# A row softmax limited by its transfers: loads of 3 to 32 rows and stores of up to 16, in place of sixteen equal chunks of 8

## The chip, the cores and the metric

The kernel runs on one core of one Trainium2 chip. The metric is device microseconds of one execution. The kernel before takes 163.15 us (median of the first 3 runs, 162.96 to 163.39). Four engines matter here: DVE (VectorE, the maxima and the scaling), ACT (ScalarE, the exponentials), the DMA engines (16 of them, which carry the loads and the stores), and SP, which only issues the loads. The stores are issued by ACT. The TensorE is not used; the granted clock was 1.0.

The profile's span is about 1.8 us shorter than the device time (161.3 us against 163.08 us in the profiled run). Times inside the program are counted from the span's start.

## The reference

```python
def setup_inputs():
    batch, seq, dim = 16, 1024, 512
    return {"x": np.random.randn(batch, seq, dim).astype(np.float32)}

def reference(x):
    x_max = np.max(x, axis=-1, keepdims=True)
    exp_x = np.exp(x - x_max)
    return (exp_x / np.sum(exp_x, axis=-1, keepdims=True)).astype(np.float32)
```

That is a softmax over 512 numbers for 16,384 rows. A core has 128 partitions, so each partition gets 128 rows of 2 KB. In all, 33.55 MB are read and 33.55 MB written. Below, "8 rows" means 8 rows in each of the 128 partitions: 2 MB in all, 16 KB per partition.

## The kernel before

```python
CHUNKS = [8] * 16
SLOTS = {8: 12}
...
    def load(k):                       # SP issues; 16 KB per partition
        tiles[k] = data.tile([P, R, d], F32, ..., bufs=SLOTS[R])
        nc.sync.dma_start(out=tiles[k], in_=src[k])

    def rowmax(k):                     # DVE: one instruction for 8 rows
        nc.vector.reduce_max(out=shift[k], in_=tiles[k], axis=AX, negate=True)

    def exps(k):                       # ACT: one instruction per row, with its sum
        for r in range(R):
            nc.scalar.activation(out=tiles[k][:, r, :], in_=tiles[k][:, r, :], func=EXP,
                bias=shift[k][:, r : r + 1], accum_out=sums[k][:, r : r + 1], ...)

    def scale(k):                      # DVE: reciprocal, then one product per row
        ...
    def store(k):                      # ACT issues
        nc.scalar.dma_start(out=dst[k], in_=tiles[k])

    with tc.manual_schedule():
        for k in range(K):
            load(k); rowmax(k); exps(k)
            if k >= 1:
                scale(k - 1); store(k - 1)
        scale(K - 1); store(K - 1)
```

Twelve chunks of 16 KB per partition, 192 KB, are held at a time.

Of the kernel before, what the change touches and what calls it, by code (L numbers as in the profile page):

```python
# [1 line left out]

# [4 lines left out]

F32 = mybir.dt.float32
EXP = mybir.ActivationFunctionType.Exp
AX = mybir.AxisListType.X  # L10


CHUNKS = [8] * 16

SLOTS = {8: 12}


@with_exitstack
def kernel(
    ctx: ExitStack,  # L20
    tc: tile.TileContext,
    x: bass.AP,
    out: bass.AP,
):
    nc = tc.nc
    P = nc.NUM_PARTITIONS

    x_flat = x.flatten_outer_dims()
    out_flat = out.flatten_outer_dims()
    n, d = x_flat.shape  # L30
    assert n == P * sum(CHUNKS)


    src, dst, at = [], [], 0
    for R in CHUNKS:
        for flat, views in ((x_flat, src), (out_flat, dst)):
            part = flat[at : at + P * R, :]
            views.append(part.rearrange("(p r) d -> p r d", r=R))
        at += P * R

    data = ctx.enter_context(tc.tile_pool(name="data", bufs=1))
    stats = ctx.enter_context(tc.tile_pool(name="stats", bufs=4))

    K = len(CHUNKS)
    tiles = [None] * K
    shift = [None] * K
    sums = [None] * K

    def load(k):
        R = CHUNKS[k]  # L50
        tiles[k] = data.tile([P, R, d], F32, name=f"x{R}", tag=f"x{R}", bufs=SLOTS[R])
        nc.sync.dma_start(out=tiles[k], in_=src[k])  # L52

    def rowmax(k):
        R = CHUNKS[k]
        shift[k] = stats.tile([P, R], F32, name=f"shift{R}", tag=f"shift{R}")
        nc.vector.reduce_max(out=shift[k], in_=tiles[k], axis=AX, negate=True)  # L57

    def exps(k):
        R = CHUNKS[k]  # L60
        sums[k] = stats.tile([P, R], F32, name=f"sums{R}", tag=f"sums{R}")
        for r in range(R):
            nc.scalar.activation(  # L63
                out=tiles[k][:, r, :],
                in_=tiles[k][:, r, :],
                func=EXP,
                bias=shift[k][:, r : r + 1],
                scale=1.0,
                accum_out=sums[k][:, r : r + 1],
            )  # L70

    def scale(k):
        R = CHUNKS[k]
        recip = stats.tile([P, R], F32, name=f"recip{R}", tag=f"recip{R}")
        nc.vector.reciprocal(out=recip, in_=sums[k])  # L75
        for r in range(R):
            nc.vector.tensor_scalar_mul(  # L77
                out=tiles[k][:, r, :],
                in0=tiles[k][:, r, :],
                scalar1=recip[:, r : r + 1],  # L80
            )

    def store(k):
        nc.scalar.dma_start(out=dst[k], in_=tiles[k])  # L84

    with tc.manual_schedule():
        for k in range(K):
            load(k)
            rowmax(k)
            exps(k)  # L90
            if k >= 1:
                scale(k - 1)
                store(k - 1)
        scale(K - 1)
        store(K - 1)


# [1 line left out]
_INS = ['x']  # L99
_OUTS = [((16, 1024, 512), 'float32')]  # L100


# [23 lines left out]
```

## Time and profile before

| | value | where it is read |
|---|---|---|
| span | 161.3 us | page |
| DMA busy | nine tenths or more in 38 of 40 slices | page, DMA row |
| DVE, ACT busy | 77%, 58% | page |
| bytes moved | 67.1 MB, about 431 GB/s in a full slice | page |
| 16 KB piece on one DMA engine | 611 ns; the next begins 607 ns after it began | the trace's DMA packets |
| last store issued | 149.49 us | timeline |

These are lines of the profile page of the kernel before: the span, two engines' busy time, the busy tenths of the DMA engines and the GB/s in 40 equal slices of 4.03 us, and the packets, MB and share of each queue (q1 the loads, q10 the stores).

```profile
span 161.3 us, 527 instructions
...
DVE 123.8 (77%) x160; ACT 93.2 (58%) x257; POOL 0.2 (0%) x4
...
DMA  6999999999999999999999999999999999999993
GB/s 163 431 427 427 431 435 378 418 445 431 423 439 431 421 435 431 431 439 418 439 435 427 431 427 435 435 425 435 431 427 439 431 427 427 431 435 431 431 435 171
...
q1 hardware_dynamic: 2304, 33.56, 49.5%
q10 hardware_dynamic: 2304, 33.56, 48.6%
```

The reader should see that the DMA engines are never without work between the first and the last slice, and that the rate is the same with loads alone (slices 2 to 6), with both, and with stores alone (the last seven). The small dip to 378 GB/s in slice 7 is where the first store joins.

The next line is the page's chain of work that ended last, by engine, as shares of the span.

```profile
DMA 52%; DVE 31%; ACT 6%; SPq 2%; issue 1%; ACTq 1%; DVEq 0%
```

The chain goes back from the last instruction, and the time that a store spends in its queue after it was issued is not one of its steps. The timeline of the kernel before shows that time; its columns are start, duration, engine, source line, operation, tiles.

```profile
22.40 0.37 ACTq L84 DMA_DIRECT2D out_dram<-x  x1
...
146.19 3.26 DVE L77 TENSOR_SCALAR x<-x,recip 128x512 f32<-128x512 f32 x8
...
149.49 0.34 ACTq L84 DMA_DIRECT2D out_dram<-x  x1
```

The last store is issued at 149.49 us and moves 2 MB, which takes 4.9 us at 431 GB/s. It does not start until about 154 us, because earlier stores are still in the queue. DVE could have ended some 3 us later without loss (an estimate: these 4.5 us, less the 1.0 us from the first load's issue to its first piece). So DVE is not the limit; the DMA engines are.

### A budget of one DMA engine

For a kernel of this kind I need a finer account than the page. The trace has one record for each piece that a DMA engine moves: start, duration, size and queue (the recorded texts below call a piece a packet). One partition's contiguous run is one piece, so a chunk of 8 rows makes 128 pieces of 16 KB, 8 on each engine. The engine's number is not recorded; I joined pieces to 16 engines by the end of one and the start of the next. A few pieces are joined wrongly (the bytes of an engine come out up to a few per cent off 4.19 MB), so the means over the 16 engines are good and a single engine's figure is approximate.

The budget has these terms, in us per engine, as means over 16, and together with the 1.74 us before the first piece they make the mean end: the usual time of all its pieces (each size's usual duration, less the 4 ns by which pieces overlap); "slow", by how much pieces took longer than is usual for their size; idle gaps; and "spread", by how much the last engine ends after the mean.

```
kernel          pieces  usual   slow   gaps   mean end  spread  last engine's end   span
before            256   155.39  1.58   0.47    159.19    0.98        160.17        161.3
```

Of the 1.58 us of slow pieces, 0.92 lie in the first 4 us and 0.53 where the first store joins at 24.6 to 28 us.

### The profile page before, as it was taken

What the parts mean: (1) busy time and instruction counts of PE and PEld (TensorE: products, weight loads), DVE (VectorE), ACT (ScalarE), POOL (GpSimd) and SP (SyncE); (2) the same over time, 40 slices, a digit from 0 to 9 for tenths busy, and PEclk for the clock granted to TensorE, in tenths of its full rate; (3) what the DMA queues carried; (4) which work ended last, traced back from release to release, by engine and by line L of the source; (5) the groups of instructions that cost most, each with busy time, mean ns of one, the idle gap of its engine ahead of it and who ended that gap; (6) DMA issues with size and microseconds to landing.
All of it is one profiled execution on the core that took longest, in us unless ns stands there. A gap on an engine that the chain in (4) does not pass through costs nothing.

```text
span 161.3 us, 527 instructions
## 1 busy us (share of the span) xinstructions
DVE 123.8 (77%) x160; ACT 93.2 (58%) x257; POOL 0.2 (0%) x4
## 2 busy tenths in 40 slices
DVE  0088799999999999985970079999999999957000
ACT  0037994959596867067002996859595959591000
POOL 0000000000000000000000000000000000000000
DMA  6999999999999999999999999999999999999993
GB/s 163 431 427 427 431 435 378 418 445 431 423 439 431 421 435 431 431 439 418 439 435 427 431 427 435 435 425 435 431 427 439 431 427 427 431 435 431 431 435 171
DMA packets 4612, 67.14 MB, mean 416 GB/s; under 512 B 513, under 2 KB 513, under 8 KB 513
## 3 DMA queue, kind: packets, MB, share of 16 engines
q1 hardware_dynamic: 2304, 33.56, 49.5%
q10 hardware_dynamic: 2304, 33.56, 48.6%
q14 instruction: 4, 0.02, 0.0%
HBM read 33.55 MB, written 33.55 MB: 416 GB/s over the span
## 4 chain that ended last, share of the span: by engine, by line
DMA 52%; DVE 31%; ACT 6%; SPq 2%; issue 1%; ACTq 1%; DVEq 0%
DMA x<-in_x_dram 52%; DVE shift L57 16%; DVE x L77 14%; ACT x L63 6%; SPq L52 2%; DVE recip L75 1%; ACTq L84 0%; DVEq L121 0%; ACTq L63 0%
## 5 line engine op out<-in xcount | busy, mean ns | idle before, releaser
L63 ACT ACTIVATE x<-x,shift 128x512 f32<-128x512 f32 x128 | 90.5, 709 | 44.1 <-DVE shift L57 21.4
L57 DVE TENSOR_REDUCE shift<-x 128x8 f32<-128x4096 f32 x16 | 70.6, 4415 | 9.7 <-DMA x<-in_x_dram 9.7
L77 DVE TENSOR_SCALAR x<-x,recip 128x512 f32<-128x512 f32 x128 | 52.1, 482 | 0.6
L63 ACT ACTIVATION_READ_ACCUMULATOR x<-x,shift 128x1 f32 x128 | 24.0, 187 | 0.0
L75 DVE RECIPROCAL recip<-sums 128x8 f32<-128x8 f32 x16 | 3.1, 196 | 15.3 <-ACT x L63 15.3
L63 ACT ACT_TABLE_LOAD x1 | 1.3, 1283 | 8.7 <-DMA x<-in_x_dram 8.7
L110 POOL MEMSET const-bfloat16-1.0<- 128x1 bf16 x1 | 0.1, 102 | 0.0
L110 POOL MEMSET const-uint8-127<- 128x1 uint8 x1 | 0.1, 102 | 0.0
L110 POOL MEMSET const-float32-0.0<- 128x1 f32 x1 | 0.1, 99 | 0.2 <-issue 0.2
L110 POOL MEMSET const-float32-1.0<- 128x1 f32 x1 | 0.1, 99 | 0.0
## 6 DMA issues: line engine op xcount, KB each, us to landing
x<-in_x_dram SPq DMA_DIRECT2D x16, 2048.0 KB, 42.6
out_dram<-x ACTq DMA_DIRECT2D x16, 2048.0 KB, 18.0
```

The costliest lines, as they stand in the source:

```text
L52: nc.sync.dma_start(out=tiles[k], in_=src[k])
L57: nc.vector.reduce_max(out=shift[k], in_=tiles[k], axis=AX, negate=True)
L63: nc.scalar.activation(out=tiles[k][:, r, :], in_=tiles[k][:, r, :], func=EXP, bias=shift[k][:, r : r + 1], scale=1.0, accum_out=sums[k][: ...
L75: nc.vector.reciprocal(out=recip, in_=sums[k])
L77: nc.vector.tensor_scalar_mul(out=tiles[k][:, r, :], in0=tiles[k][:, r, :], scalar1=recip[:, r : r + 1],)
L110: nc = _bacc.Bacc("TRN2", target_bir_lowering=False, num_devices=1)
```

## The change

The intent is to start computing and storing earlier (a first load of 3 rows), to move the bulk in fewer, larger transfers, and to hold everything in one array of 192 KB per partition, whose first 32 rows are reused by the last two chunks.

```diff
-CHUNKS = [8] * 16
-SLOTS = {8: 12}
+CHUNKS = [   # rows, place in the array
+    (3, 0), (5, 3), (8, 8), (16, 16), (32, 32), (32, 64), (16, 0), (16, 16),
+]
+SBUF_ROWS = 96
+EARLY = 6                             # loads issued at the start
+AFTER_STORE = {2: [6], 3: [7]}        # load 6 after the store of chunk 2, 7 after 3
+GROUP = 8                             # rows computed at a time
+FINISH_BEFORE = (1, 2, 3)             # chunks 0 to 2 are finished before the next begins
+STORE_ROWS = {4: 16, 5: 16}           # the 32-row chunks are stored by 16
 ...
+    held = data.tile([P, SBUF_ROWS, d], F32, name="held")
+    place = [held[:, s : s + R, :] for R, s in CHUNKS]
 ...
     def load(k):
-        tiles[k] = data.tile([P, R, d], F32, ..., bufs=SLOTS[R])
-        nc.sync.dma_start(out=tiles[k], in_=src[k])
+        nc.sync.dma_start(out=place[k], in_=src[k])
 ...        # rowmax, exps and scale now work on a group g of 8 rows (or 3, or 5)
+        if since is not None:         # end of the group: rows since..b are stored
+            nc.scalar.dma_start(out=dst[k][:, since:b, :], in_=place[k][:, since:b, :])
+        if b == CHUNKS[k][0]:
+            for later in AFTER_STORE.get(k, ()):
+                load(later)
 ...
+        for k in range(EARLY):
+            load(k)
+        waiting = None
+        for g, (k, a, _, _) in enumerate(groups):
+            if waiting is not None and a == 0 and k in FINISH_BEFORE:
+                scale(waiting)
+                waiting = None
+            rowmax(g)
+            exps(g)
+            if waiting is not None:
+                scale(waiting)
+            waiting = g
+        scale(waiting)
```

The compute is the same but for one more maximum and one more reciprocal. Comments in this diff are mine.

## The prediction

> **What bounds the kernel now.** The DMA engines, end to end. In the page's 40 slices the DMA row reads 9 in all but the first and last, at about 431 GB/s, whether loads, stores or both are moving. It moves 67.1 MB: 155.5 of 161.3 us. DVE is busy 77%, ACT 58%. A 16 KB packet begins 607 ns after the one before on its engine; 256 per engine make 155.4 us. The rest: first packet at 1.74 us, about 0.9 us of slow first packets, 0.5 us of slow packets where the first store joins (25 to 26.5 us), 1.3 us to the last landing, 0.8 us to the end. Loads end at 132 us; then a backlog of stores drains: the last (2 MB) is issued at 149.5 us (timeline) and starts near 154 us.
>
> The long waits (ACT 12.1 us for a load, whose semaphore a store reuses) cost nothing: the DMA was never without work.
>
> **What the change does.** Same bytes, same 192 KB, nearly the same DVE and ACT work. It removes packets: loads of up to 64 KB and stores of up to 32 KB per partition, 144 instead of 256 per engine. It moves the first store from 22.4 us to about 11.3 us (3 rows land near 5.6, maximum 1.75, exps 2.1, scale 1.4); that fills no hole, as loads fill the engines then. It adds: chunks 0 to 3 run one by one, so 16 rows are done at about 34 us (before: some 20); loads 6 and 7 wait for stores; the last store is 4 MB, 9.7 us instead of 4.9.
>
> The Trainium skill ("DMA: Bandwidth & Descriptors", section "Where 436 GB/s comes from") gives a ceiling of 435 GB/s; the trace shows 431 to 432. 16 KB at the ceiling is 602 ns, so a packet's own cost is an estimated 5 ns: 112 fewer save an estimated 0.55 us, all critical.
>
> **Is DVE still in time?** An estimate from its durations: 7.735 us for 8 rows (timeline, 97 to 140 us), 16 rows at 34 us, so last maximum ends near 137.3 us (before 140.1), last store issued near 146.8 us. By then the DMA, if never idle, nears row 224 of 256 (loads plus stores), which ends near 148.5 us; a first packet comes 1.0 us or more after issue. The last store arrives just in time, margin about 1 us. The first 32-row load must also beat the small stores: the same page ("Queues, rings and completion order") says engines alternate between queues per packet, and the trace shows load, store, load, store. With 64 KB load packets against 6 to 10 KB stores it lands near 46 us, needed at 47.8. If split into 32 KB, near 50, and DVE ends 2 us later.
>
> **Prediction.** 162.5 us, range 161.3 to 164.6: a gain of about 0.6 us, the risk lying above. Faster by over 2% 0.05, within 2% 0.89, slower 0.06.
>
> **Right or wrong, in the profile.** DMA row 9 throughout, 431 to 435 GB/s; first store issued at 11 to 12 us; DVE ends at 146 to 149 us; no dip before the last store.
>
> **What would make it wrong.** A rate that depends on packet size (64 KB strides in HBM); a dip between 65 and 90 us where loads 6 and 7 wait; the one-by-one start; the last store late by several us.

## The result, and the profile after

The changed kernel takes 164.49 us (median of 4 runs, 164.45 to 164.67) against 163.17 us (4 runs). The ratio is 1.0083, with a 95% interval of 1.0065 to 1.0100. A ratio in this document is worked out from the fast runs of both kernels in the same rounds, so it is not quite the ratio of the medians. The change is thus 0.8% slower: within 2%, but of the opposite sign to the forecast.

The same lines of the page after (the slices are 4.07 us here), with the chain's shares in the last line:

```profile
span 162.7 us, 510 instructions
...
DVE 124.0 (76%) x162; ACT 93.3 (57%) x257; POOL 0.2 (0%) x4
...
DMA  5999997979889799899999999999999999999991
GB/s 203 433 475 387 402 559 311 561 333 543 335 356 540 330 403 542 346 387 467 403 403 379 395 475 419 397 483 411 427 451 411 459 435 395 475 427 395 475 419 56
...
q1 hardware_dynamic: 1152, 33.55, 49.3%
q10 hardware_dynamic: 1440, 33.56, 48.0%
...
DVE 55%; DMA 28%; ACT 3%; issue 3%; SPq 1%; DVEq 0%; ACTq 0%
```

Two readings are traps. First, the chain of waits went from DMA 52% to DVE 55%, as if DVE had become the limit. It had not: DVE's busy time is the same (124.0 against 123.8 us), and the last store is issued earlier than before. Second, the GB/s row jumps between 311 and 561. A 64 KB piece takes 2.4 us on one engine and is counted whole in one slice, so this row cannot be read for such pieces. If each piece's bytes are spread over its own duration, the rate between 24 and 36 us is 429 to 433 GB/s.

Here is the timeline after: the first store, the only longer wait of DVE for a load once it is under way, and the end.

```profile
10.74 0.37 ACTq L103 DMA_DIRECT2D out_dram<-held  x1
...
48.72 4.42 DVE L75 TENSOR_REDUCE shift<-held 128x8 f32<-128x4096 f32 x1 [2.01 <-DMA held<-in_x_dram]
...
144.27 3.26 DVE L97 TENSOR_SCALAR held<-held,recip 128x512 f32<-128x512 f32 x8
...
147.56 0.34 ACTq L103 DMA_DIRECT2D out_dram<-held  x1
```

The first store comes 11.7 us earlier than before, and the last one 1.9 us earlier. The engines are not idle before it: its first pieces start at 149.5 us, right behind the store ahead of it. Compute is not what got slower.

The budget shows where the time went:

```
kernel          pieces  usual   slow   gaps   mean end  spread  last engine's end   span
before            256   155.39  1.58   0.47    159.19    0.98        160.17        161.3
after             144   154.83  2.77   0.46    159.80    1.65        161.45        162.7
difference       -112   -0.56  +1.19  -0.01     +0.61   +0.67         +1.28         +1.4
```

The saving that the change is made for, fewer pieces, is there: 0.56 us. It is more than eaten by slow pieces (+1.19 us per engine) and by the spread of the engines' ends (+0.67 us). The slow time, by period: 0.42 us in the first 8 us (before: 0.92 in the first 4), 0.34 at 12 to 24 us, 0.16 at 32 to 40, 0.44 at 40 to 48, 0.21 at 56 to 64, 0.41 at 76 to 84 and 0.66 at 84 to 88 us. It lies on load pieces almost alone (2.51 of 2.77 us), and nearly all of it comes before 88 us, while the loads go on to 117 us.

This listing, made from the trace's DMA packets, shows three of the engines at 82 to 89 us. L is a piece of a load and S one of a store, with its size in KB and its start; the bracket is by how many ns it was slow; a point is the small write that reports a transfer done.

```
L32@81.2 S32@82.4 L32@83.6 . L32@84.9(+631) S32@86.7 L32@87.9 S32@89.1
S32@82.0 L32@83.2 S32@84.4 L32@85.6(+802) S32@87.6 L32@88.8
S32@82.1 L32@83.3 S32@84.5 L32@85.7(+1318) . L32@88.3 S32@89.5
```

All the engines stall over the same two or three microseconds, but not by the same amount. Since each engine has its own fixed 4.19 MB to move, an engine that stalls more stays behind to the end. When the records are joined so that each piece is followed by the one that starts nearest to 4 ns before its end, 12 of the 16 engines come out at exactly 144 pieces. In this joining the two engines that end near 161.4 us have 3.6 and 3.8 us of slow pieces, and the eleven that end before 159.7 us have 2.2 to 2.6 us. So in the changed kernel the spread is not a second cause: it is the same slow time, unevenly shared.

What makes pieces slow? Three theories went into the experiments. A: the large load pieces. B: the order of work (small chunks first, one by one; late loads 6 and 7). C: the late 4 MB last store. Theory A was sharpened on the way; the letters D to G stand for theories that the recorded expectations below name.

### The profile page after: what moved, and what is told of

It is laid out like the page before. It is cut to its first block, busy times and chain, and to the rows that moved or that the text cites. A ratio compares the mean times of both kernels' runs of the same rounds, so it can differ in the third digit from the quotient of the medians.

```text
span 162.7 us, 510 instructions
## 1 busy us (share of the span) xinstructions
DVE 124.0 (76%) x162; ACT 93.3 (57%) x257; POOL 0.2 (0%) x4
## 4 chain that ended last, share of the span: by engine, by line
DVE 55%; DMA 28%; ACT 3%; issue 3%; SPq 1%; DVEq 0%; ACTq 0%
DVE shift L75 30%; DMA held<-in_x_dram 28%; DVE held L97 24%; ACT held L83 3%; SPq L70 1%; DVE recip L95 1%; DVEq L149 0%; ACTq L83 0%
## 5 line engine op out<-in xcount | busy, mean ns | idle before, releaser
L83 ACT ACTIVATE held<-held,shift 128x512 f32<-128x512 f32 x128 | 90.5, 708 | 45.5 <-DVE shift L75 39.6
L75 DVE TENSOR_REDUCE shift<-held 128x8 f32<-128x4096 f32 (+2 forms) x17 | 70.6, 4159 | 7.2 <-DMA held<-in_x_dram 7.2
L97 DVE TENSOR_SCALAR held<-held,recip 128x512 f32<-128x512 f32 x128 | 52.2, 480 | 0.6
L83 ACT ACTIVATION_READ_ACCUMULATOR held<-held,shift 128x1 f32 x128 | 23.9, 187 | 0.0
L95 DVE RECIPROCAL recip<-sums 128x8 f32<-128x8 f32 (+2 forms) x17 | 3.3, 192 | 15.8 <-ACT held L83 15.8
```

The costliest lines, as they stand in the source:

```text
L75: nc.vector.reduce_max(out=shift[g], in_=place[k][:, a:b, :], axis=AX, negate=True)
L83: nc.scalar.activation(out=place[k][:, r, :], in_=place[k][:, r, :], func=EXP, bias=shift[g][:, r - a : r - a + 1], scale=1.0, accum_out=s ...
L95: nc.vector.reciprocal(out=recip, in_=sums[g])
L97: nc.vector.tensor_scalar_mul(out=place[k][:, r, :], in0=place[k][:, r, :], scalar1=recip[:, r - a : r - a + 1],)
```

## The experiments

All runs below gave correct results. "Slow" and "spread" are the terms of the budget in the run that was profiled.

```
kernel      median us  ratio to before    pieces  slow   gaps   spread  last engine
before       163.15                         256   1.58   0.47    0.98     160.17
after        164.49   1.0083                144   2.77   0.46    1.65     161.45
l8           171.84   1.0533                216   2.62   8.82    0.10     168.44
s8           166.39   1.0201                200   2.60   0.57    3.85     163.87
ls8          163.08   0.9997                272   1.52   0.58    0.73     159.99
b35          163.21   1.0004                272   1.62   0.52    0.90     160.22
l16          162.69   0.9979                160   1.18   0.60    0.97     159.42
start8       164.83   1.0105                128   2.82   0.45    2.12     161.89
nodry        165.31   1.0135                160   2.62   0.59    2.46     162.32
bsplit       163.52   1.0024                264   1.90   0.57    1.07     160.71
cut5         164.49   1.0084                152   2.13   0.54    1.92     161.18
cut4         163.29   1.0017                152   1.58   1.00    0.89     160.06
l16dry       162.60   0.9973                160   1.33   0.49    1.00     159.43
l16start8    162.56   0.9967                144   1.49   0.79    0.69     159.53
first64      164.56   (one look)            104   1.77   3.17    0.10     161.42
best8        162.64   0.9967                152   1.50   0.45    0.98     159.53
best35       162.95   0.9980                168   1.45   0.46    1.25     159.83
best64       162.38   0.9959                112   1.64   0.45    0.83     159.33
best64b      162.89   0.9985                128   2.29   0.36    0.92     160.06
small64      163.96   1.0052                128   3.03   0.38    2.41     162.33
```

Some cautions. The ratios' intervals are about 0.0013 wide to each side. Only l8 is slower by a clear 2%; s8 lies at that limit, and all the other differences are smaller. The runs were made on four chips, each beside the kernel before, whose medians there lay between 163.06 and 163.13 us. And the profiled run of small64 was the slowest of its six (165.25 us against a median of 163.96), so its slow and spread terms together are about 1.3 us too large for a typical run. l16start8 and best8 each had one execution near 167 us, which the ratios leave out as slow.

### 1. Cut the loads, the stores, or both to 8 rows

The edits to the changed kernel: for the loads,

```diff
-        nc.sync.dma_start(out=place[k], in_=src[k])
+        for a in range(0, R, 8):
+            b = min(R, a + 8)
+            nc.sync.dma_start(out=place[k][:, a:b, :], in_=src[k][:, a:b, :])
```

and for the stores `STORE_ROWS = {3: 8, 4: 8, 5: 8, 6: 8, 7: 8}`. Run l8 has the first, s8 the second, ls8 both.

> Changed kernel, with every load cut into pieces of at most 8 rows (16 KB packets); memory layout, order, stores untouched. Budget of one DMA engine so far: packets slower than the usual time of their size cost 1.58 us in the kernel before and 2.77 us in the changed one; the last engine ends 0.98 us after the mean of the 16 before and 1.65 us after. Theory A (large load packets cause the slow packets): they fall to 1.0 to 1.6 us, packets' own cost rises 0.35 us, time about 163.5 us. Rival B (order of work, small first chunks, late loads are the cause): slow packets stay near 2.7, time 164.5 +-0.3 us.

> Changed kernel, with every store cut to at most 8 rows (16 KB packets); loads keep 32 KB and 64 KB packets. Theory A: slow packets of the loads stay (2.3 us or more per engine), the spread of the engines' ends falls from 1.65 to about 1.0 us, time about 163.9 us. Rival B: both stay, 164.5 +-0.3 us. Rival C (the 4 MB last store is issued too late): time falls as well, but then the trace should show the store queue empty before the last store.

> Changed kernel, loads and stores both cut to at most 8 rows; array, places, DRAM layout, order of compute untouched. Theory A: slow packets about 1.0 to 1.6 us and spread about 1.0 us per engine, time 162.7 to 163.2 us, that is as before or a little better. Rival B: 164.5 +-0.3 us. Rival D (64 KB stride between partitions in DRAM, not packet size, makes the loads slow): slow packets stay at 2.3 us or more, time near 164.2 us.

Measured: 171.84, 166.39 and 163.08 us. Each half of the edit does harm, and both together bring back the time of the kernel before. Theory A had forecast the time of ls8 (162.7 to 163.2 us), but no theory had forecast that each half alone does harm. B is out as the main cause, because ls8 has the small chunks, the order and the late loads of the changed kernel and is 1.4 us faster. D is out too: ls8 reads with the same 64 KB stride between partitions, and is not slow.

l8 shows what inequality can do in the extreme. The engines alternate between the two queues piece by piece (between 60 and 70 us, 93% of the joined pieces follow one of the other queue), so 16 KB loads beside 32 KB stores get about one third of the engine. Between 64 and 68 us the pieces show 135 GB/s of loads and 297 GB/s of stores (in the kernel before: 248 and 183). The loads fall behind and DVE has to wait for them, here in l8's timeline:

```profile
135.37 4.42 DVE L78 TENSOR_REDUCE shift<-held 128x8 f32<-128x4096 f32 x1 [3.87 <-DMA held<-in_x_dram]
...
143.87 4.42 DVE L78 TENSOR_REDUCE shift<-held 128x8 f32<-128x4096 f32 x1 [0.67 <-DMA held<-in_x_dram]
...
154.39 3.26 DVE L100 TENSOR_SCALAR held<-held,recip 128x512 f32<-128x512 f32 x8
```

and the stores that wait for DVE leave the DMA engines empty. The view by windows of l8 gives start and end, length, busy time of DVE, ACT and POOL with counts, the clock, the DMA's busy share and its GB/s:

```profile
128.00:136.00 8.00, 4.10 (x11) 5.75 (x16) 0.00 (x0) 1.00 0.99 428
...
140.00:144.00 4.00, 3.33 (x9) 4.00 (x11) 0.00 (x0) 1.00 0.18 78
```

That is the 8.8 us of gaps in the table, and it explains l8's time. It is not what happens in the changed kernel, which has no such gaps.

s8 is the opposite case: 64 and 32 KB loads beside 16 KB stores. Its engines always have work (gaps 0.57 us), it is slow to the same amount as the changed kernel (2.60), but its last engine ends 3.85 us after the mean. Why its spread is more than twice that of the changed kernel at about the same slow time is not shown. Theory C finds nothing there: the stores run without a break to the end.

### 2. The small start in the kernel before

Run b35 gives the kernel before the chunks 3, 5 and fifteen of 8; run bsplit cuts only its first load into 3 and 5 rows.

```diff
-CHUNKS = [8] * 16                 # b35
+CHUNKS = [3, 5] + [8] * 15
-        nc.sync.dma_start(out=tiles[k], in_=src[k])      # bsplit
+        for a, b in ((0, 3), (3, 8)) if k == 0 else ((0, R),):
+            nc.sync.dma_start(out=tiles[k][:, a:b, :], in_=src[k][:, a:b, :])
```

> Kernel before, with its first 8-row chunk cut into 3 and 5 rows, nothing else. The slow packets of the first 4 us cost 0.92 us per engine before and 0.42 us with the changed kernel's small first loads. If small first packets are the reason, this gives 162.6 to 162.8 us. If the small stores that follow disturb the stream, or the 3 and 5 row start does nothing by itself, 163.2 us or more.

> Kernel before with its first load cut into 3 and 5 rows, its chunk and its store left whole. The kernel before with 3 and 5 row chunks won 0.44 us per engine in the first 4 us and lost 0.43 us where three small first stores, not one, joined. If that is so, the win is kept here: slow packets 1.1 us per engine instead of 1.58, time 162.6 to 162.8 us, under both kernels. If not, 163.1 us.

Measured: 163.21 and 163.52 us, no gain. In b35 the slow pieces of the start fall from 0.92 to 0.48 us, but 1.01 us appear at 12 to 28 us. In bsplit the start costs 0.64 us, and the one first store, unchanged in size and moment, now costs 1.15 instead of 0.53 us. So my expectation for bsplit was wrong: what is won at the start is lost when the store queue joins. Start and first stores together cost 1.5 to 1.8 us in the kernel before and in these two. Why is not shown.

### 3. No load piece over 32 KB

Run l16 cuts the two 32-row loads of the changed kernel into pieces of 16 rows (the loop above with 16 for 8); cut5 does it for the second alone, cut4 for the first alone.

> Changed kernel with its two 32-row loads cut into pieces of 16 rows, so that no load packet is over 32 KB, as no store packet is; all else as changed. Theory A1 (it is the inequality of load and store packets: 64 KB loads beside small stores): slow packets from 36 to 62 us (0.9 us per engine with the changed kernel) go, those at 77 to 87 us (1.0 us), where both are 32 KB, stay; 163.7 to 164.2 us. Theory A2 (size of load packets as such): both shrink, 163.3 us. Rival: loads get a smaller share against the first stores, the second 16-row piece lands late, DVE waits, and time rises over 164.7 us.

> Changed kernel, only the second of its two 32-row loads cut into 16-row pieces (no cut: 164.49 us; both cut: 162.69 us). Theory A2 (each 64 KB load packet stream does its own harm): about half of the gain, 163.3 to 163.9 us, with the slow packets of 43 to 47 us (0.44 us per engine) kept and those of 58 to 62 us gone. Rival E (what matters is only that loads 6 and 7 are issued before the load queue runs empty): time follows the moment of load 6's issue; if the queue still runs empty, 164.2 us or more.

> Changed kernel, only the first of its two 32-row loads cut into 16-row pieces. Theory A2: 163.3 to 163.9 us, slow packets of 43 to 47 us gone or halved. Rival E: as for the other half; the first store lands earlier than in the changed kernel, so load 6 is issued earlier, and if the load queue then does not run empty the time is near 162.7 us although one 64 KB load is left.

Measured: l16 takes 162.69 us, 1.8 us less than the changed kernel and faster than the kernel before (0.9979, interval 0.9965 to 0.9992). Slow pieces fall from 2.77 to 1.18 us and the spread to 0.97 us. Even those at 77 to 87 us are gone, where both the changed kernel and l16 move 32 KB loads beside 32 KB stores. I had expected them to stay, so they look like an after-effect of the 64 KB pieces before them; no run shows that by itself.

Cutting the second of the two 64 KB loads alone changes nothing (cut5, 164.49 us, with 0.43 us at 43 to 47 us kept), so one load of 64 KB pieces beside a small store is enough for the whole loss. By the times of the pieces, that first 32-row load (23.8 to 48 us) runs beside the store of 5 rows (28.6 to 49 us, pieces of 10 KB); the store of 3 rows is over at 24.9 us. Cutting the first alone gives 163.29 us. This does not show that the second load is harmless beside a small store: in cut4 it moves at 51.4 to 78.9 us, when the store of 8 rows is over at 52.6 us, and so it meets the 32 KB pieces of the next store instead.

### 4. The order: the start of 8, and a load queue that runs empty

Run start8 joins the first two chunks of the changed kernel to one of 8 rows. nodry loads chunk 6 in two halves, so that the load queue does not run empty at 72 us. l16dry is l16 with loads 6 and 7 both held back until chunk 3 is stored, which was meant to make the load queue run empty. l16start8 is l16 with the start of 8.

```diff
-    (3, 0), (5, 3), (8, 8), (16, 16), ...      # start8, l16start8
+    (8, 0), (8, 8), (16, 16), ...              # and the indices that follow from it
-    ... (32, 64), (16, 0), (16, 16),           # nodry
+    ... (32, 64), (8, 0), (8, 8), (16, 16),
-AFTER_STORE = {2: [6], 3: [7]}
+AFTER_STORE = {1: [6], 2: [7], 3: [8]}
-    ... (32, 64), (16, 0), (16, 16),           # l16dry
+    ... (32, 64), (16, 16), (16, 0),
-AFTER_STORE = {2: [6], 3: [7]}
+AFTER_STORE = {3: [6, 7]}
```

> Changed kernel with its first two chunks (3 and 5 rows) joined to one of 8. If the 6 and 10 KB stores among 64 KB loads make the slow packets of 13 to 47 us, those (about 1.1 us per engine) fall by half or more, while the slow first 4 us return (0.9 instead of 0.4 us): 164.0 us. If they don't matter, slow packets rise by 0.5 us: 164.9 us. The last store is issued about 1 us earlier or at the same time (147.5 us), which decides nothing.

> Changed kernel with the load of chunk 6 (16 rows) cut into two chunks of 8, of which the first waits for the stores of the first 8 rows alone (landed at 51.5 us), so that the queue of loads does not run empty at 72 us, as it does in the changed kernel. If a restart of an empty load queue makes the slow packets of 77 to 80 us (0.41 us per engine), they go, and perhaps those of 83 to 87 us (0.66) too: 163.5 to 164.1 us. If not, 164.5 +-0.3 us.

> The fast version (loads of at most 16 rows, 162.69 us), with the places of the last two chunks exchanged, so that load 6 waits for the store of chunk 3 (landed at 78 us) while the loads before it end at about 66 us: the load queue runs empty for some 12 us on purpose, with no packet over 32 KB. Rival E: slow packets of 0.5 to 1.0 us per engine return where it restarts, and the time is 163.5 us or more. Theory A2: nothing over 0.3 us returns, 162.6 to 163.0 us.

> The fast version with its first two chunks (3 and 5 rows) joined to one of 8. In the fast version the first 8 us cost 0.29 us per engine in slow packets, in the kernel before 0.92. If the small start is worth that difference there, 163.2 us; if the first stores of 6 and 10 KB cost as much elsewhere (0.65 us per engine from 12 to 36 us), 162.7 us: the small start is then worth nothing.

Measured: 164.83, 165.31, 162.60 and 162.56 us. A load queue that runs empty is not the cause, but l16dry cannot show it. Its edit did not do what was meant: the second half of chunk 5 was still being loaded at 66.0 to 85.2 us when loads 6 and 7 were issued at 78 us, so the load queue never ran empty. Other runs settle it. In cut5 and nodry the load queue does not run empty, and they are no faster than the changed kernel. In best64 (section 5) no load piece moves from 67.9 to 75.8 us, next to nothing is slow from 66 to 90 us (0.03 us), and best64 has the lowest time of all. In nodry the slow pieces at 77 to 80 us go, but 0.93 us come at 100 to 104 us, and the time is worse; nodry also puts 16 KB loads beside 32 KB stores, so how much worse it is does not belong to the queue alone. The small start is worth nothing either: l16start8 has 0.90 us of slow pieces in its first 4 us against 0.29 us of l16 in its first 8, less at the first stores, and the same time. In start8 the 64 KB loads run beside two stores of 16 KB instead of one of 10 and one of 16 KB. I had written 164.0 us if stores of 6 and 10 KB did special harm, and 164.9 us if not; so beside 64 KB loads the store of 10 KB is no worse than one of 16 KB.

### 5. 64 KB pieces without small stores beside them

Run first64 puts three chunks of 32 rows first, so that 64 KB load pieces run alone until stores of 32 KB pieces join. best64 adds that the last 16 rows are stored in two pieces of 8; best64b also cuts the first load into 8, 8 and 16 rows, so that DVE starts earlier. small64 is best64 with one thing changed: chunk 0 is stored by 8 rows instead of 16.

```diff
-    (3, 0), (5, 3), (8, 8), (16, 16), (32, 32), (32, 64), (16, 0), (16, 16),
+    (32, 0), (32, 32), (32, 64), (16, 0), (16, 16),
-EARLY = 6;  AFTER_STORE = {2: [6], 3: [7]};  FINISH_BEFORE = (1, 2, 3)
+EARLY = 3;  AFTER_STORE = {0: [3, 4]};       FINISH_BEFORE = ()
-STORE_ROWS = {4: 16, 5: 16}
+STORE_ROWS = {0: 16, 1: 16, 2: 16}             # first64
+STORE_ROWS = {0: 16, 1: 16, 2: 16, 4: 8}       # best64
+STORE_ROWS = {0: 8, 1: 16, 2: 16, 4: 8}        # small64
```

> Changed kernel with its chunks in another order: the two 32-row loads and a third come first, so that 64 KB load packets run alone until a first store of 16 rows (32 KB packets) at some 45 us. It is meant to be slow (DVE starts at about 22 us instead of 5: 175 us or more) and is read for its slow packets alone. Theory F (64 KB packets are slow beside stores of another size, not as such): under 0.1 us per engine between 5 and 40 us, more after the first store. Theory G (64 KB packets are slow by themselves, for instance by their stride in DRAM): 0.3 us or more per engine spread over 5 to 40 us.

> The kernel with 32-row loads first (164.56 us in one look), with its last 16 rows stored in two pieces of 8. There every engine stood idle for 2.80 us at 148 to 152 us before the last store, the ends of the engines lay within 0.2 us, and no packet was slow but at the start and before the first store. If the idle time was the late last store alone, it goes: 161.6 to 162.0 us, faster than both kernels. If the last piece of 8 is still late, 162.5 us or more.

> The same, with the first 32-row load cut into 8, 8 and 16 rows, so that DVE starts near 9 us instead of 23 and has 10 us in hand at the end. If only the last store's lateness matters, as fast as or faster than the other, 161.4 to 162.0 us. Its first stores (32 KB packets) meet more of the 64 KB loads: theory F (inequality of packets) allows some slow packets and a spread of the ends of up to 1 us, 162.0 to 162.8 us.

> The same as the first, with the stores of chunk 0 in four pieces of 8 rows (16 KB packets) instead of two of 16: the one difference is small stores beside 64 KB loads. Theory F: slow packets rise by 0.5 us per engine or more after the first store, the ends of the engines spread to 1 us or more, time 0.8 us or more over the first. Rival (order and early small chunks did the harm, packets did not): within 0.3 us of the first.

first64 took 164.56 us in its one look (a single run, whose state is not known, so it is read for its slow pieces rather than for its time), where I had written 175 or more. I had not worked that out from the 7.735 us that DVE needs for 8 rows: sixteen times that after a load that lands at 22.7 us gives 147 us for DVE, and its last store was issued at 150.66 us. As to what it was made for, it is clear. From 8 to 44 us, with 64 KB pieces alone, the pieces show 433 to 434 GB/s and nothing slow; theory G is out (best64 below shows the same in its profile). With stores of 32 KB beside them (52 to 68 us) the rate stays at 433 to 434 GB/s. Slow are only the start (0.74 us) and the moment when the first store joins (0.84 us). The engines end within 0.2 us of each other. What spoils its time is the last store, in first64's timeline:

```profile
136.96 0.34 ACTq L103 DMA_DIRECT2D out_dram<-held  x1
...
150.66 0.34 ACTq L103 DMA_DIRECT2D out_dram<-held  x1
```

and in its windows, where the last two columns are again the DMA's busy share and GB/s:

```profile
138.00:148.00 10.00, 7.46 (x13) 7.11 (x20) 0.00 (x0) 1.00 0.99 426
...
148.00:152.00 4.00, 2.63 (x7) 0.00 (x0) 0.00 (x0) 1.00 0.34 147
```

The DMA engines are idle for 2.8 us before the last store. With the last 16 rows in two stores, best64, the timeline is

```profile
136.82 0.34 ACTq L103 DMA_DIRECT2D out_dram<-held  x1
...
144.55 0.34 ACTq L103 DMA_DIRECT2D out_dram<-held  x1
...
150.53 0.34 ACTq L103 DMA_DIRECT2D out_dram<-held  x1
```

the gap is gone (0.45 us of gaps in all), and the page of best64 reads

```profile
span 160.6 us, 494 instructions
...
DMA  7969969969989999999999999999999999999993
```

(the digits below 9 at the start are again 64 KB pieces counted whole in one slice). Its 162.38 us are the lowest median: 0.9959 of the kernel before (interval 0.9946 to 0.9971), though not clear of l16start8 and best8 (both 0.9967). My 161.6 to 162.0 was a little too hopeful, since the spread rose from 0.10 to 0.83 us in the profiled run. Starting DVE earlier (best64b) gains nothing, as the engines are never idle in best64. It meets more of the 64 KB loads with stores, has 1.56 us of slow pieces at 28 to 40 us, and takes 162.89 us.

small64 is the narrowest comparison. Its only edit to best64 is that 32 rows are stored as four pieces of 8 rows instead of two of 16. It takes 163.96 us, 1.6 us more. The last stores are issued at the same moments (144.63 and 150.59 us against 144.55 and 150.53 us), and the gaps are no larger (0.38 against 0.45 us). In small64's timeline the four stores of chunk 0 and the last two stores are

```profile
36.41 0.38 ACTq L103 DMA_DIRECT2D out_dram<-held  x1
...
44.14 0.34 ACTq L103 DMA_DIRECT2D out_dram<-held  x1
...
51.88 0.34 ACTq L103 DMA_DIRECT2D out_dram<-held  x1
...
59.60 0.34 ACTq L103 DMA_DIRECT2D out_dram<-held  x1
...
144.63 0.34 ACTq L103 DMA_DIRECT2D out_dram<-held  x1
...
150.59 0.34 ACTq L103 DMA_DIRECT2D out_dram<-held  x1
```

Slow pieces rise from 1.64 to 3.03 us and the spread from 0.83 to 2.41 us, with the caution given above about the profiled run. Of the slow time, 1.16 us lie where the first store joins (0.94 in best64) and 0.83 us at 104 to 108 us, 12 us after the last piece of the small stores (91.6 us). So storing these 32 rows in pieces of 16 instead of 32 KB costs the 1.6 us; in the profiled run it shows as slow pieces, some of them 12 us and more after the small stores. Of the four small stores only the first ran beside 64 KB loads throughout (42.2 to 62.1 us); the fourth ran beside 32 KB loads (76.2 to 91.6 us), and the run does not tell which of them did the harm. That something is left behind which causes the later ones is my reading, and no run isolates it. The edit cannot be made without also making the first store come 8 us earlier (36.4 instead of 44.1 us); best64b, whose first store comes at 30.5 us in 32 KB pieces, is 1.1 us faster than small64, so the earlier moment alone does not seem to explain it, though best64b also cuts its first load.

### 6. The last store in two pieces, with loads of at most 16 rows

```diff
+STORE_ROWS = {3: 16, 4: 16, 6: 8}       # best8: l16start8 so
+STORE_ROWS = {4: 16, 5: 16, 7: 8}       # best35: l16 so
```

> Loads of at most 16 rows, first chunk of 8 rows (162.56 us), and now the last 16 rows stored in two pieces of 8. In the version without it the engines were idle for 0.32 us each at 148 to 152 us, as the last store was issued at 148.1 us. If that wait is real it goes: 162.2 to 162.4 us. If the last store was in time, 162.5 to 162.7 us.

> Loads of at most 16 rows, first chunks of 3 and 5 rows (162.69 us), and the last 16 rows stored in two pieces of 8. Here the trace showed no idle engines before the last store (issued at 147.4 us), so nothing should come of it: 162.5 to 162.8 us.

Measured: 162.64 and 162.95 us. best8 was to gain 0.2 to 0.4 us and gained nothing, although its gaps fell from 0.79 to 0.45 us. A gap of 0.3 us that most engines share need not be on the path of the last engine: the mean end moved from 158.84 to 158.56 us, the last engine's end stayed at 159.53 us. For best35 nothing was expected, and nothing came (0.9980 against l16's 0.9979, from other rounds). Neither is distinguishable from l16 and l16start8.

## Why the prediction was wrong, point by point

**What bounds the kernel.** Right. In every run without gaps the time is the last DMA engine's end plus 1.1 to 1.4 us to the span's end. Waits of ACT and DVE moved without effect.

**Fewer pieces save an estimated 0.55 us.** Right: the usual time of all pieces fell by 0.56 us, from 155.39 to 154.83 us. A 64 KB piece took 2418 ns, a 32 KB piece 1213 ns and a 16 KB piece 611 ns, each less a 4 ns overlap, so 434.4, 433.7 and 431.9 GB/s. The Trainium skill ("DMA: Bandwidth & Descriptors", section "Where 436 GB/s comes from") gives 435 GB/s as the ceiling, and no size exceeded it.

**The rest stays as it is.** This is the step that failed. The prediction listed "0.9 us of slow first packets, 0.5 us of slow packets where the first store joins" and "1.3 us to the last landing", in which the spread of about 1 us is contained, and carried them over unchanged into "a gain of about 0.6 us". The start shrank to 0.42 us, but the other slow pieces grew from 0.66 to 2.35 us and the spread from 0.98 to 1.65 us. It treated the time of a piece as a constant of its size. In the kernel before, with 16 KB pieces in both queues, that held from 28 us on (0.12 us of slow pieces); in the changed kernel, with 64 KB loads beside stores of 10 and 16 KB, it did not.

**Alternation by packet.** The prediction used it for one question only, whether the first 32-row load lands in time. It estimated 46 us and needed 47.8; the load landed at 48.7 us and DVE waited 2.0 us. The pieces stayed whole at 64 KB. This was one of the places where the harm began (0.44 us of slow pieces at 40 to 48 us), but the wait itself cost nothing.

**DVE in time for the last store.** Right. Issued at 147.56 us (predicted 146.8, range 146 to 149), first piece at 149.5 us, no idle time before it. The first store at 10.74 us was a little earlier than forecast.

**"No dip before the last store", "DMA row 9 throughout".** Wrong as a test: the page's row is not readable with 2.4 us pieces, and the dips that exist (358 GB/s at 84 to 88 us with bytes spread over their pieces) are stalls, not idle time.

**What would make it wrong.** "64 KB strides in HBM" is refuted by ls8 and first64. The "dip between 65 and 90 us" came, at the place named, but not for the reason named: best64's load queue was empty for 7.9 us at no cost, and keeping it filled in cut5 and nodry did not help.

What stays open is why a piece becomes slow. The runs show when: at the start, when the first store joins, and, with 64 KB loads beside stores of 10 to 16 KB, several times more, up to some 30 us after the last such store (in nodry that store ended at 73.3 us, and pieces were slow at 100 to 104 us). They show that stores of 16 rows instead of 8 remove most of what comes after the first store has joined (1.2 us in small64, 0.1 us in best64), and that cutting the loads to 32 KB removes it as well (l16). They do not show which part of the chip stalls; the trace has no record of that.

## What to carry to other kernels

When loads and stores share the DMA engines, choose the contiguous run per partition for both queues together: loads and stores of 16 and 16 KB, 32 and 32, 64 and 32 worked here, and so did 32 KB loads beside stores of 10 and 16 KB (l16), so equality is not needed. Kernels with 64 KB loads beside stores of 10 to 16 KB took 0.9 to 3.3 us more than the kernel before, and 16 KB loads beside 32 KB stores, where DVE had to wait, 8.7 us more. For a kernel that is bound by its transfers, keep a budget of one DMA engine (usual time, slow pieces, gaps, and how much later the last engine ends than the mean): a saving in one term can come back in another without any wait showing in the compute engines. Merge transfers only as far as the term that it saves is worth, here 0.56 us, and keep the last store small enough that it is issued before the queue ahead of it is empty.

## What the Trainium skill lacked or had wrong

- "DMA: Bandwidth & Descriptors", section "Queues, rings and completion order", says that an engine goes round its queues packet by packet, a packet being typically 9 to 17 descriptors. The trace agrees on the alternation, but the unit here was one partition's run, of 6 to 64 KB. The page does not say what follows: the queues' shares of the bandwidth go by the size of that run. 16 KB loads beside 32 KB stores got 135 GB/s against 297 GB/s.
- "SBUF — State Buffer", section "The DMA setup-cost knee", has the rule to "coalesce into the largest single transfer you can". From 2 MB to 8 MB per load the rate of a piece rose only from 431.9 to 434.4 GB/s, and what the 8 MB loads were worth hung on the stores beside them, of which the rule says nothing: with small stores the kernel was 0.8% slower (164.49 us), with stores of 32 KB pieces, in best64, 0.4% faster (162.38 us), and with loads of at most 4 MB 0.2% faster (162.69 us).
- No page tells of slow pieces at a transition: 0.92 us per engine at the start and 0.53 us when the first store joins in the kernel before, and 2.35 us after the first 8 us in the changed kernel.
- "DMA: Bandwidth & Descriptors", section "Why a DMA increments its semaphore by 16 and not by 1", says that the engines of one transfer finish independently, without a size. From the first to the last of the 16 small writes that report a transfer done took 0.8 to 2.6 us in the kernel before and up to 5.4 us in the changed one.
- The same page, section "Latency and other measured facts", gives about 0.6 us to the first byte. The page does not say from where that is counted. From the end of the issuing instruction the trace agrees for idle engines: in the kernel before, the first load's first piece came 0.64 us after it (0.73 + 0.37 us, to 1.74 us). The page has no figure for a queue that joins while the other is at work: the first store's first piece came 3.7 to 4.0 us after its issue began beside loads of 16 and 32 KB pieces (10.74 to 14.48 us in the changed kernel, 10.67 to 14.67 us in l8), and 4.3 to 5.8 us after it beside 64 KB pieces (best64b and small64).
